# Output-projection weights prepared in the first MLP's second product instead of at the end of attention

## The chip, the cores and the metric

The kernel runs on one core of one Trainium2 chip. The metric is device microseconds of one execution: 2729.65 us in the median of three runs (2724.99 to 2732.59). One further execution was profiled. All times below are microseconds from the start of that execution's span unless they are called times of runs.

## The reference

Two post-norm residual layers over x of 1024 tokens x 1024 channels, f32. Layer 0 mixes tokens with a chunked gMLP, layer 1 with dilated attention in three patterns; each is followed by a squared-ReLU MLP. Every part is modulated by a conditioning vector c.

```python
for i in range(DEPTH):                      # DEPTH = 2
    shift, scale, gate = ada_mod(c, ada_w[i, 0], ada_b[i, 0])
    h = x * (1.0 + scale) + shift
    y = mixer_a(h, ...) if i == 0 else mixer_b(h, w_qkv, w_out, slopes)
    x = layer_norm(ALPHA * x + gate * y, ln_g[i, 0], ln_b[i, 0])
    shift, scale, gate = ada_mod(c, ada_w[i, 1], ada_b[i, 1])
    h = x * (1.0 + scale) + shift
    y = jnp.square(jax.nn.relu(h @ w_up)) @ w_down
    x = layer_norm(ALPHA * x + gate * y, ln_g[i, 1], ln_b[i, 1])

def mixer_b(h, w_qkv, w_out, slopes):       # 16 heads of 64, patterns (128,1) (512,4) (2048,16)
    ...
    outs, lses = one dilated_branch per pattern
    wts = softmax(stack(lses), axis=0)[..., None]
    o = sum(wts * stack(outs), axis=0)      # the merge
    return o.reshape(B, S, 1024) @ w_out
```

`w_out` of layer 1 (1024 x 1024) is what the change is about. Since `gate * (o @ w_out)` is `o @ (w_out * gate)`, its columns can be multiplied by the gate row beforehand.

## The kernel before

**Products.** Each f32 product runs as three matmuls of a rounded part (hi) and a rest (lo): hi x hi, hi x lo, lo x hi. An operand is split by `split`: ScalarE (ACT) casts to hi (line 102), VectorE (DVE) subtracts to get lo (line 103). The MLPs' products are cut into quarters and combined into seven products.

**Stages**, by the timeline: conditioning and gMLP mixer until about 365; first MLP, up product (psua to psuc) until 678.9; its second product (psd, line 955) until about 975; projection of the values (psv) until 1377; attention until 2033; the rest of the output projection (psoc, psod, psoe) until 2096; second MLP until the end.

**The second product of an MLP** (in `mlp`, with `load_step`, `prepare` and `matmuls`) is a loop over 56 steps of 24 matmuls (7 products x 8 pairs of k). Loads are issued three steps ahead, splits (lhi, llo of the left operand, rhi, rlo of the right one) two steps ahead. In between DVE takes up other work: differences of weight blocks that are held (heldt, heldr), and the residual acc, which is read back and multiplied and added to by the norm's rows (lines 300, 301). `x_tile` hands out 128x512 buffers from a ring.

**Attention** treats the 16 heads as 8 pairs (hp) x 3 patterns (g = 2, 1, 0): 24 groups of 8 slots, each slot of two half slots. A function decorated with `at(slot, pos, rank)` or passed to `in_half` is called when the planner comes to that half slot; between these calls matmuls of the q and k projections (psq, psk) and, at the end, of the output projection (psoa, psob) are dealt out. Per group: scores sc (line 1447), maxima and exponentials p (1467, 1469), transposes pT (1500), split into pThi and pTlo, product with the values pv (1527), evicted and added to oT (1536, 1537).

**The merge** of a pair joins its three patterns. `factors` computes weights from the maxima and sums (mm, ma, mal, lines 1590 to 1602) and stores them (w_dram), `spread` reads them back over the partitions as rows bc, and small steps scale (1623), add (1627) and cut (split into oTs, the left operand of the output projection). The last pair's merge runs in `go_on`, between psoc's and psod's matmuls; psod's last matmuls of each group (k = 7) and psoe need it.

**The output projection's weights** are 8 units of 128 x 1024 (wo). `staged_unit` loads one raw, multiplies it by the gate row (DVE, 1712), and splits it (ACT 102, DVE 103), for units 0 to 5 at set slots near the end of attention, for 6 and 7 in `go_on`.

**Order.** Every engine works through its own queue in order. SP's queue issues most DMAs; POOL's issues a few; an instruction that waits holds up what is behind it on its queue. A scheduler may move instructions on an engine, except those marked `tc.keep_in_program_order` ("pinned"), which keep their order among themselves.

Of the kernel before, what the change touches and what calls it, by code (L numbers as in the profile page):

```python
# [35 lines left out]
def trunk(ctx: ExitStack, tc: tile.TileContext, x, c, ada_w, ada_b, ln_g, ln_b, a_w_in, a_b_in,  # L36
# [615 lines left out]

    LEFT = {1: 0, 2: 1, 4: 2, 5: 3, 6: 4, 7: 5, 3: 6}
# [9 lines left out]
    def mlp(j, before, ahead=iter(())):  # L663
# [14 lines left out]
        with ExitStack() as ph:  # L678
# [324 lines left out]

            last_p = order[-1]
# [4 lines left out]
            with ExitStack() as pa:  # L1009
# [5 lines left out]
                for n, (p, kp) in enumerate(steps):  # L1015
# [35 lines left out]
                    if n == 4 * NT and j == 3:  # L1051
                        res.affine(j)
                    if p == last_p and kp > 0:
                        next(between, None)
# [3 lines left out]
                for m in range(4):  # L1058
                    for kp in range(tail, KP):
                        matmuls(last_p, kp, ms=[m], pinned=True)  # L1060
                    evict(last_p, m)()
                    res.finish(m, (1,))
                    if j == 3:
                        res.result(m, m == 3)
            spsum.close()
# [206 lines left out]
    def attention(form):  # L1272
# [5 lines left out]
        with ExitStack() as ph:  # L1278
# [104 lines left out]
            def attend(n, oT_of):  # L1383
# [6 lines left out]
                @at(base + 1, 0)  # L1390
# [178 lines left out]
            def merge(hp, oTs):  # L1569
# [15 lines left out]
                @at(*((base + 4, 0) if hp < N_PAIRS - 1 else (base + 1, 0)))  # L1585
                def factors():
# [3 lines left out]
                    in_order(V.tensor_tensor(m[:], nm[:, 0], nm[:, 1], op=ALU.min))  # L1590
# [15 lines left out]
                @at(*((base + 4, 1) if hp < N_PAIRS - 1 else (base + 1, 0)))  # L1606
# [39 lines left out]
                for n, f in enumerate(steps):  # L1646
                    n = pace * n + 18
                    at(base + n // 2, n % 2)(f)
# [44 lines left out]
            def pinned_split(hi, lo, src):  # L1693
                for x_ in split(hi, lo, src):
                    tc.keep_in_program_order(x_)

            @at(last_group - 13, 0)
            def gate_row():
                ending["gate"] = vec.tile([P, D], F32, name="gate_2", tag="oT", bufs=4)
                nc.sync.dma_start(ending["gate"][:], gate_dram[2].partition_broadcast(P))  # L1700

            def staged_unit(k, load, gate, ready):
                box = {}

                @at(last_group + load[0], load[1])
                def load_raw():
                    box["raw"] = wts.tile([P, D], F32, name=f"wo_{k}_raw", tag="raw", bufs=2)
                    nc.sync.dma_start(box["raw"][:], b_w_out[0, k * P : (k + 1) * P, :])

                @at(last_group + gate[0], gate[1])  # L1710
                def apply_gate():
                    tc.keep_in_program_order(V.tensor_tensor(box["raw"][:], box["raw"][:], ending["gate"][:], op=ALU.mult))

                def split_raw():
                    hi, lo = (wts.tile([P, D], F32R, name=f"wo_{k}_{m}", tag=f"w{m}")[:] for m in ("hi", "lo"))
                    pinned_split(hi, lo, box["raw"][:])
                    ending["units"][k] = hi, lo

                if ready is None:
                    return split_raw  # L1720
                at(last_group + ready[0], ready[1])(split_raw)

            staged_unit(0, (-14, 0), (-12, 0), (-11, 0))
            staged_unit(1, (-13, 0), (-11, 1), (-10, 1))
            staged_unit(2, (-11, 0), (-10, 0), (-9, 0))
            staged_unit(3, (-10, 1), (-9, 1), (-8, 0))
            staged_unit(4, (-2, 0), (2, 0), (8, 0))
            staged_unit(5, (-1, 0), (4, 0), (8, 1))
            late = [staged_unit(6, (9, 0), (11, 1), None), staged_unit(7, (9, 1), (12, 1), None)]
# [48 lines left out]
            def go_on():  # L1778
# [4 lines left out]
                for f in late:  # L1783
                    f()
# [73 lines left out]
```

## Time and profile before

| what | value |
|---|---|
| runs | 2729.65 us median (2724.99 to 2732.59), 3 runs |
| the profiled execution's own time | 2727.96 us |
| its span | 2726.2 us, 36911 instructions |
| mean granted TensorE clock | 0.995 |
| PE busy | 2658.8 us, 98% |
| DVE, ACT busy | 1989.8 us (73%), 1377.1 us (51%) |
| DMA | 487.98 MB, mean 179 GB/s |

The span runs from the first to the last instruction; 1.8 us of the execution lie around it. Busy shares are averages over stages that differ, so the prediction reads stretches of 25 us, and in them the idle time of PE. A row of a timeline gives start, duration, engine, line, operation, output<-inputs and, in brackets, how long the engine stood idle before it and what ended that. A row of the chain gives start, duration and the work on the path that ended last. bc, wo, pTlo and the like are the program's tile names.

### The profile page before, as it was taken

How to read it: one execution, taken by the hardware profiler on the slowest of the kernel's cores; microseconds unless marked ns; L12 is line 12 of the kernel's file. 1: busy time of each engine (PE TensorE's matmuls, PEld its weight loads, DVE VectorE, ACT ScalarE, POOL GpSimd, SP SyncE). 2: the span in 40 equal slices, each digit the busy share in tenths (PEclk: the TensorE clock that was granted, in tenths of full speed). 3: DMA queues.
4: the chain of work that ended last, by engine and by line, in shares of the span. 5: the costliest groups of instructions: out<-in, count | busy, mean ns of one | idle time of the engine just before them, and what ended most of it. 6: DMA issues, size and time to landing. Idle time of an engine off the chain costs nothing.

```text
span 2726.2 us, 36911 instructions
## 1 busy us (share of the span) xinstructions
PE 2658.8 (98%) x13242; PEld 2196.3 (81%) x13242; DVE 1989.8 (73%) x3594; ACT 1377.1 (51%) x2593; POOL 97.0 (4%) x161
## 2 busy tenths in 40 slices
PE   6999999999999999999999999999999999999998
PEld 5788888887888878888888888888777788878886
DVE  6787698787867778555557767777768966577877
ACT  3354375555443464434436666666655655554332
POOL 1000000000000000111110000000010000000000
PEclk9999999999999999999999999999999999999999
DMA  7534346667936545655565554555672654485562
GB/s 263 159 118 134 116 140 224 227 214 257 333 131 194 195 155 193 212 186 182 178 210 153 155 140 129 132 144 139 193 183 105 202 189 159 149 311 192 171 207 86
DMA packets 332572, 487.98 MB, mean 179 GB/s; under 512 B 50988, under 2 KB 176340, under 8 KB 332388
## 3 DMA queue, kind: packets, MB, share of 16 engines
q1 hardware_dynamic: 318564, 435.29, 50.3%
q0 software_dynamic: 13824, 50.34, 5.2%
q8 instruction: 104, 1.70, 0.3%
q14 instruction: 80, 0.66, 0.1%
HBM read 357.01 MB, written 128.53 MB: 178 GB/s over the span
## 4 chain that ended last, share of the span: by engine, by line
PE 77%; DVE 12%; DMA 6%; ACT 3%; issue 2%; SPq 1%; DVEq 0%; ACTq 0%
PE psd L955 22%; PE psv L1257 13%; PE psua L796 7%; PE psq L1358 6%; PE psk L1358 6%; DMA adaw<-in_ada_w_dram 3%; PE psuc L796 3%; PE psd_wout L389 3%; PE psu L368 3%; PE pv L1527 3%; PE sc L1447 2%; PE psv L470 2%; PE psub L796 2%; DVE adaacc L128 1%; DVE left L103 1%
## 5 line engine op out<-in xcount | busy, mean ns | idle before, releaser
L796 PE MATMUL psua<-right,left 128*128 128x512 f32 x1536 | 363.4, 390 | 0.3
L955 PE MATMUL psd<-rhi,lhi 128*128 128x512 f32 x896 | 349.9, 390 | 3.0 <-ACT part L827 3.0
L955 PE MATMUL psd<-rlo,lhi 128*128 128x512 f32 x896 | 349.6, 390 | 0.2
L955 PE MATMUL psd<-rhi,llo 128*128 128x512 f32 x896 | 349.2, 390 | 0.0
L796 PEld LDWEIGHTS psua<-right,left 128*128 128x128 f32 x1536 | 287.1, 188 | 61.7 <-DVE right L103 1.4
L1469 ACT ACTIVATE p<-p,stat 128x128 f32<-128x128 f32 (+1 forms) x384 | 168.7, 441 | 107.8 <-DVE stat L1467 104.7
L955 PEld LDWEIGHTS psd<-rhi,lhi 128*128 128x128 f32 x896 | 168.6, 188 | 39.1 <-ACT part L827 3.9
L955 PEld LDWEIGHTS psd<-rlo,lhi 128*128 128x128 f32 x896 | 168.5, 188 | 35.9 <-DVE rlo L103 1.1
L955 PEld LDWEIGHTS psd<-rhi,llo 128*128 128x128 f32 x896 | 168.6, 188 | 35.0
L796 PE MATMUL psuc<-right,left 128*128 128x512 f32 x768 | 187.2, 390 | 0.0
L128 DVE SCALAR_TENSOR_TENSOR adaacc<-adaw,silu_c,adaacc 128x512 f32<-128x512 f32 x168 | 128.5, 775 | 55.0 <-DMA adaw<-in_ada_w_dram 54.6
L796 PEld LDWEIGHTS psuc<-right,left 128*128 128x128 f32 x768 | 143.5, 188 | 30.0 <-DVE right L103 0.4
L103 DVE TENSOR_TENSOR pTlo<-pT,pThi 128x512 fp32r<-128x512 f32 (+1 forms) x160 | 99.3, 621 | 75.1 <-ACT pThi L102 74.1
L103 DVE TENSOR_TENSOR left<-ws,left 128x512 fp32r<-128x512 f32 x128 | 87.8, 688 | 71.5 <-ACT left L102 69.7
L103 DVE TENSOR_TENSOR llo<-lraw,lhi 128x1024 fp32r<-128x1024 f32 x112 | 136.4, 1218 | 0.8 <-ACT lhi L102 0.8
L102 ACT CAST left<-ws 128x512 fp32r<-128x512 f32 x128 | 79.1, 620 | 99.1 <-DVE ws L717 87.8
L1358 PE MATMUL psk<-form_L,wqk_hi 128*128 128x512 f32 x384 | 127.0, 412 | 0.0
L1358 PE MATMUL psq<-form_L,wqk_hi 128*128 128x512 f32 x384 | 126.4, 410 | 0.0
L102 ACT CAST rhi<-rraw 128x1024 fp32r<-128x1024 f32 x48 | 50.6, 1053 | 139.6 <-issue 113.7
L1257 PE MATMUL psv<-vrhi,form_S 128*128 128x512 f32 x384 | 119.9, 390 | 0.6 <-ACT vrhi L102 0.4
L102 ACT CAST lhi<-lraw 128x1024 fp32r<-128x1024 f32 x112 | 117.4, 1048 | 3.5 <-PE psua L796 3.5
L1467 DVE CUSTOM_DVE_ANT_0 p<-sc,bias 128x128 f32<-128x128 f32 (+1 forms) x384 | 113.6, 346 | 6.7 <-PE sc L1447 5.8
(326 smaller groups left out, 6094.4 us busy)
## 6 DMA issues: line engine op xcount, KB each, us to landing
lraw<-forms SPq DMA_DIRECT2D x112, 512.0 KB
adaw<-in_ada_w_dram SPq DMA_DIRECT2D x192, 256.0 KB
up<-in_mlp_w_up_dram SPq DMA_DIRECT2D x64, 512.0 KB
forms<-s SPq DMA_DIRECT2D x128, 256.0 KB
rraw<-in_mlp_w_down_dram SPq DMA_DIRECT2D x64, 512.0 KB
forms<-part SPq DMA_DIRECT2D x96, 256.0 KB
v<-vs POOLq DMA_DIRECT2D x48, 512.0 KB, 3.7
vraw<-in_b_w_qkv_dram SPq DMA_DIRECT2D x42, 512.0 KB
```

The lines of the kernel that those rows point to most:

```text
L102: first = A.copy(hi, src) if hi_engine is A else hi_engine.tensor_copy(hi, src)
L103: return first, lo_engine.tensor_tensor(lo, src, hi, op=ALU.subtract)
L128: ins = V.scalar_tensor_tensor(acc[:], raw[:], silu_c[:, k : k + 1], acc[:], ALU.mult, ALU.add)
L368: T.matmul(dst, s[a], m[b], start=(n == 0), stop=(n == last))
L389: T.matmul(p[:], stat[a][:, k, o : o + P], u[b][:, w], start=n == 0, stop=n == count - 1)
L796: T.matmul(acc, w[:, a, k, :], right[p][:, b, k, :], start=p in (1, 2, 5) and k + a + b == 0, stop=k == 3 and a == 1, skip_group_check=True)
L955: ins = T.matmul(sums[kind, m][:], l[a][:, k, m * P : (m + 1) * P], r[b][:, k, :], start=p in (1, 5, 2, 3) and kp + k + a + b == 0, stop=k ...
L1257: T.matmul(acc, rows[:, m * P : (m + 1) * P], cols_, start=p in (1, 2, 5) and kp + k + a + b == 0, stop=kp == 1 and k == 1 and a == 1, ski ...
L1358: T.matmul(p[:], wu[a][:, k * P : (k + 1) * P], h_op(k, half, b), start=k + c_ == 0, stop=k == KD - 1 and c_ == 2)
L1467: V.tensor_tensor_reduce(out=pr, in0=banks[e][:, sl], in1=st["bias"][:, width - w :], scale=-0.125, scalar=3e38, op0=ALU.add, op1=ALU.min, ...
L1469: A.activation(pr, pr, AF.Exp, bias=nm, scale=-1.0, accum_out=l)
L1527: T.matmul(pvs[b][:, q0 % HALF : q0 % HALF + w_], stt, x_[:, o_ : o_ + w_], start=not begun[b], stop=left[b] == 0, skip_group_check=True)
```

## The change

1. **Weights.** `output_weights`, called in each step of the first MLP's second product, treats the output weights in 16 halves (pieces) of 128 x 512: a load into an `x_tile`, two or more steps later the multiplication by the gate row (pinned), the split, and two stores by POOL's queue to a DRAM buffer `wo_parts`. One piece starts every 2.75 steps or so, from step 3 on. The gate row is loaded once as two half rows.
2. **Units.** In attention, `load_unit` replaces `staged_unit`: it reads hi and lo of a unit, already split, from `wo_parts` (2 x 512 KB), at half slots before and in the last group; unit 3 into the tiles of the raw projection weights, unit 7 into a tile of the values, the others into the split weights' tiles.
3. **Values.** `load_v` is called two slots earlier.
4. **Merge.** The scale, add and cut steps of pairs 0 to 6 come four half slots later.
5. **Last merge.** `factors` and `spread` of pair 7 are called one half slot later, and the first operation of every `factors` is pinned.

```diff
+    wo_dram = dram.tile([N_PAIRS, P, 2, 2, HALF], F32, name="wo_parts")
...
+            across, pieces, begun = [], deque((k, dh) for k in range(N_PAIRS) for dh in range(2)), deque()
+            def output_weights(n):
+                if n == 1:
+                    for dh in range(2):
+                        across.append(work.tile([P, HALF], F32, name=f"gate_2_{dh}", tag="h"))
+                        nc.sync.dma_start(across[dh][:], gate_dram[2, dh * HALF : (dh + 1) * HALF].partition_broadcast(P))
+                if n > 2 and pieces and (n - 2) * 16 // 44 > N_PAIRS * 2 - len(pieces) - 1:
+                    k, dh = pieces.popleft()
+                    raw = x_tile(f"wo_raw_{k}_{dh}")
+                    nc.sync.dma_start(raw[:], b_w_out[0, k * P : (k + 1) * P, dh * HALF : (dh + 1) * HALF])
+                    begun.append((n, k, dh, raw))
+                elif begun and begun[0][0] < n - 1:
+                    _, k, dh, raw = begun.popleft()
+                    hi = x_tile(f"wo_hi_{k}_{dh}")
+                    tc.keep_in_program_order(V.tensor_tensor(raw[:], raw[:], across[dh][:], op=ALU.mult))
+                    split(hi[:].bitcast(F32R), raw[:].bitcast(F32R), raw[:])
+                    for i, t in enumerate((hi, raw)):
+                        nc.gpsimd.dma_start(wo_dram[k, :, dh, i, :], t[:])
...
+                    if j == 1:
+                        output_weights(n)
...
-                @at(base + 1, 0)
+                @at(max(0, base - 1), 0)
                 def load_v():
...
-                @at(*((base + 4, 0) if hp < N_PAIRS - 1 else (base + 1, 0)))
+                @at(*((base + 4, 0) if hp < N_PAIRS - 1 else (base + 1, 1)))
                 def factors():
...
-                    in_order(V.tensor_tensor(m[:], nm[:, 0], nm[:, 1], op=ALU.min))
+                    tc.keep_in_program_order(V.tensor_tensor(m[:], nm[:, 0], nm[:, 1], op=ALU.min))
...
-                @at(*((base + 4, 1) if hp < N_PAIRS - 1 else (base + 1, 0)))
+                @at(*((base + 4, 1) if hp < N_PAIRS - 1 else (base + 1, 1)))
                 def spread():
...
-                    n = pace * n + 18
+                    n = pace * n + 22
...
-            def staged_unit(k, load, gate, ready):
...
-            staged_unit(0, (-14, 0), (-12, 0), (-11, 0))
...
-            late = [staged_unit(6, (9, 0), (11, 1), None), staged_unit(7, (9, 1), (12, 1), None)]
+            def load_unit(k):
+                if k == 7:
+                    t = qp.tile([P, 2, D], F32R, name="wo_7", tag="v")
+                    ending["units"][k] = tuple(t[:, i, :] for i in range(2))
+                else:
+                    ending["units"][k] = tuple(wts.tile([P, D], F32R, name=f"wo_{k}_{m}", tag="raw" if k == 3 else f"w{m}", bufs=2 if k == 3 else 4)[:] for m in ("hi", "lo"))
+                for i, t in enumerate(ending["units"][k]):
+                    nc.sync.dma_start(t.rearrange("p (d c) -> p d c", c=HALF).bitcast(F32), wo_dram[k, :, :, i, :])
+
+            for k, half_slot in ((3, -34), (0, -32), (1, -30), (2, -27), (4, -15), (7, 11), (5, 17), (6, 18)):
+                in_half(2 * last_group + half_slot, 4)(lambda k=k: load_unit(k))
```

What this moves on the engines is shown at three places. Names carry their indices: oT_7_2 is pair 7, pattern 2; pTlo_15_2_0 head 15, pattern 2, part 0; bc_6_2 the factors of pair 6 for pattern 2; the long number behind is a tile's count.

DVE, where pair 6 is merged while pair 7's pattern 1 begins (1963 to 1977 in the profile), before:

```order
L1623 TENSOR_TENSOR bc_6_2_18240<-oT_6_2_17475,bc_6_2_18240 128x512 x2
L1537 TENSOR_TENSOR oT_7_2_18445<-oT_7_2_18445,pv_14_2_0_18316 64x512
L1537 TENSOR_TENSOR oT_7_2_18445<-oT_7_2_18445,pv_14_2_1_18317 64x512
L103 TENSOR_TENSOR pTlo_15_2_0_18451<-pT_15_2_0_18426,pThi_15_2_0_18450 128x512
L1467 ISA p_14_1_3_18454,stat_7_1_18332<-sc_14_1_1_18431,bias_14_1_18333 128x256
L1467 ISA stat_7_1_18332 128x1
L1467 ISA p_15_1_3_18457,stat_7_1_18332<-sc_15_1_1_18432,bias_15_1_18335 128x256
L1467 ISA stat_7_1_18332 128x1
L1712 TENSOR_TENSOR wo_2_raw_18254<-wo_2_raw_18254,gate_2_18135 128x1024
L103 TENSOR_TENSOR wo_1_lo_18288<-wo_1_raw_18137,wo_1_hi_18287 128x1024
L1623 TENSOR_TENSOR bc_6_1_18237<-oT_6_1_17766,bc_6_1_18237 128x512
L103 TENSOR_TENSOR wo_2_lo_18297<-wo_2_raw_18254,wo_2_hi_18296 128x1024
```

and after:

```order
L1563 TENSOR_TENSOR oT_7_2_18566<-oT_7_2_18566,pv_14_2_1_18444 64x512
L103 TENSOR_TENSOR pTlo_15_2_0_18572<-pT_15_2_0_18547,pThi_15_2_0_18571 128x512
L1493 ISA p_14_1_3_18575,stat_7_1_18458<-sc_14_1_1_18552,bias_14_1_18459 128x256
L1493 ISA stat_7_1_18458 128x1
L1493 ISA p_15_1_3_18578,stat_7_1_18458<-sc_15_1_1_18553,bias_15_1_18461 128x256
L1493 ISA stat_7_1_18458 128x1
L1493 ISA p_14_1_5_18581,stat_7_1_18458<-sc_14_1_1_18552,bias_14_1_18459 128x256
L1493 ISA stat_7_1_18458 128x1
L1493 ISA p_15_1_5_18584,stat_7_1_18458<-sc_15_1_1_18553,bias_15_1_18461 128x256
L1493 ISA stat_7_1_18458 128x1
L1649 TENSOR_TENSOR bc_6_2_18382<-oT_6_2_17607,bc_6_2_18382 128x512 x2
L1563 TENSOR_TENSOR oT_7_2_18566<-oT_7_2_18566,pv_15_2_0_18604 64x512
```

The scaling of pair 6 (bc_6_2) stood ahead of pTlo_15_2_0 and now stands behind it and two more rounds of p; the weights' multiply and splits are gone.

DVE, the last pTlo operations of attention and the factors of the last merge (2024 to 2033), before:

```order
L103 TENSOR_TENSOR pTlo_15_0_0_19016<-pT_15_0_0_19010,pThi_15_0_0_19015 128x512
L1590 TENSOR_TENSOR mm_7_19082<-mst_7_18992 128x16
L1591 TENSOR_TENSOR mm_7_19082<-mm_7_19082,mst_7_18992 128x16
L1594 TENSOR_TENSOR ma_7_19085<-mm_7_19082,mst_7_18992 128x16 x3
L1597 TENSOR_TENSOR mal_7_19090<-ma_7_19085,mst_7_18992 128x48
...
L103 TENSOR_TENSOR pTlo_15_0_1_19042<-pT_15_0_1_19031,pThi_15_0_1_19041 128x512
L1600 RECIPROCAL mal_7_19090<-mal_7_19090 128x16
L103 TENSOR_TENSOR wo_4_lo_19046<-wo_4_raw_18613,wo_4_hi_19045 128x1024
L103 TENSOR_TENSOR pTlo_15_0_2_19061<-pT_15_0_2_19055,pThi_15_0_2_19060 128x512
L103 TENSOR_TENSOR wo_5_lo_19065<-wo_5_raw_18637,wo_5_hi_19064 128x1024
L103 TENSOR_TENSOR pTlo_15_0_3_19079<-pT_15_0_3_19074,pThi_15_0_3_19078 128x384
L1602 TENSOR_TENSOR ma_7_19085<-ma_7_19085,mal_7_19090 128x16 x3
```

and after:

```order
L103 TENSOR_TENSOR pTlo_15_0_0_19136<-pT_15_0_0_19130,pThi_15_0_0_19135 128x512
L1563 TENSOR_TENSOR oT_7_0_19156<-oT_7_0_19156,pv_14_0_1_19071 64x512
L103 TENSOR_TENSOR pTlo_15_0_1_19162<-pT_15_0_1_19151,pThi_15_0_1_19161 128x512
L103 TENSOR_TENSOR pTlo_15_0_2_19177<-pT_15_0_2_19171,pThi_15_0_2_19176 128x512
L1563 TENSOR_TENSOR oT_7_0_19156<-oT_7_0_19156,pv_15_0_0_19165 64x512
L103 TENSOR_TENSOR pTlo_15_0_3_19195<-pT_15_0_3_19190,pThi_15_0_3_19194 128x384
L1616 TENSOR_TENSOR mm_7_19206<-mst_7_19112 128x16
L1617 TENSOR_TENSOR mm_7_19206<-mm_7_19206,mst_7_19112 128x16
L1620 TENSOR_TENSOR ma_7_19209<-mm_7_19206,mst_7_19112 128x16 x3
```

The splits of weight units 4 and 5 are gone from between the pTlo operations, and the whole computation of the factors follows the last pTlo.

At the same place SP's queue after the change (wo_parts is the new DRAM buffer, up the second MLP's weights):

```order
L1608 DMA mst_7_19112<-st_dram_11367 128x4x8
L1726 DMA wo_5_lo_19181<-wo_parts_107 128x2x512
L1726 DMA wo_5_hi_19180<-wo_parts_107 128x2x512
L1726 DMA wo_6_hi_19198<-wo_parts_107 128x2x512
L1726 DMA wo_6_lo_19199<-wo_parts_107 128x2x512
L1630 DMA w_dram_11368<-ma_7_19209 128x2x8 x3
L1637 DMA bc_7_1_19225<-w_dram_11368 64x1024 x2
```

Where four unit loads of 512 KB now stand ahead of the factors' store, there were two loads of raw weights of 512 KB (units 6 and 7).

DVE in the second product, about its seventh step, after the change (gate_2 is the gate row, wo_raw_0_0 the first piece, llo and rlo the operands' splits):

```order
L103 TENSOR_TENSOR llo_1_5_0_6327<-lraw_1_5_0_6281,lhi_1_5_0_6326 128x1024
L300 TENSOR_TENSOR acc_1_6_6021<-acc_1_6_6021,lng_0_6137 128x1024
L301 TENSOR_TENSOR acc_1_6_6021<-acc_1_6_6021,lnb_0_6139 128x1024
L103 TENSOR_TENSOR rlo_1_5_0_6332<-heldt_1_0_6031,rhi_1_5_0_6331 128x1024
L1022 TENSOR_TENSOR wo_raw_0_0_6220<-wo_raw_0_0_6220,gate_2_0_6146 128x512
L103 TENSOR_TENSOR llo_1_5_1_6378<-lraw_1_5_1_6322,lhi_1_5_1_6377 128x1024
L103 TENSOR_TENSOR wo_raw_0_0_6220<-wo_raw_0_0_6220,wo_hi_0_0_6335 128x512
L719 TENSOR_TENSOR heldt_1_0_6031<-heldr22_1_0_6033,heldt_1_0_6031 128x1024
```

The multiply and the lo part of a piece stand between the operands' splits; before, the same rows stood there without L1022 and the split of wo_raw.

30 lines of the change are left out of this document (1 added, 29 removed).

## The prediction

> **What bounds the kernel now.** I read the page's busy shares first, then the busy time of each engine in 25 us stretches, the waits of PE and DVE in the attention stage, the chain that ended last, and last the timelines of PE, DVE and SP at the places found.
>
> ```profile
> PE 2658.8 (98%) x13242; PEld 2196.3 (81%) x13242; DVE 1989.8 (73%) x3594; ACT 1377.1 (51%) x2593; POOL 97.0 (4%) x161
> ```
>
> PE is busy for 98% of the span, so no change can win more than the few tens of us in which PE is idle or runs at a reduced clock. The stretches say where these are (columns: us; busy PE, PEld, DVE, ACT, POOL; granted clock; DMA share; GB/s).
>
> ```profile
> 700.00:725.00 25.00, 25.00 (x112) 20.71 (x111) 23.86 (x22) 11.24 (x14) 0.00 (x0) 1.00 0.93 325
> 725.00:750.00 25.00, 25.00 (x112) 20.67 (x111) 23.95 (x22) 8.97 (x9) 0.00 (x0) 1.00 0.93 323
> 775.00:800.00 25.00, 25.00 (x112) 20.71 (x111) 12.54 (x11) 8.40 (x9) 0.00 (x0) 1.00 0.30 100
> 850.00:875.00 25.00, 25.00 (x112) 20.65 (x111) 24.77 (x28) 8.60 (x9) 0.00 (x0) 1.00 0.59 185
> ...
> 1475.00:1700.00 225.00, 221.84 (x1492) 185.32 (x1491) 159.79 (x487) 141.31 (x420) 7.10 (x19) 1.00 0.53 142
> 1925.00:1950.00 25.00, 25.00 (x182) 21.31 (x181) 14.28 (x56) 14.41 (x47) 0.60 (x2) 1.00 0.63 183
> 1950.00:1975.00 25.00, 20.41 (x130) 16.66 (x128) 20.48 (x51) 15.63 (x45) 0.81 (x2) 0.93 0.80 241
> 1975.00:2000.00 25.00, 22.69 (x128) 18.68 (x127) 15.31 (x40) 12.97 (x36) 3.46 (x5) 0.93 0.93 238
> 2025.00:2050.00 25.00, 22.79 (x102) 18.57 (x101) 21.66 (x38) 7.92 (x12) 0.85 (x1) 0.86 0.61 141
> ```
>
> The first four rows lie in the first MLP's second product: PE never pauses, while DVE and the DMA engines are close to full until 750. The last four lie at the end of attention. There PE loses 3.16 us in 1475 to 1700, 4.59 + 2.31 = 6.9 us in 1950 to 2000 and 2.21 us in 2025 to 2050. A mean clock of 0.93 over 25 us is 3.5 us at half rate, so up to 1.75 us lost in each of two stretches; 0.86 is 7 us at half rate, 3.5 us lost. Who is waited for (engine, line, releaser: us in total, times, longest; DVE first, then PE):
>
> ```profile
> DVE bc L1623 <- DMA bc<-w_dram: 16.2, 6, 3.7
> ...
> PE pv L1527 <- DVE pTlo L103: 7.6, 10, 2.3
> PE pv L1527 <- ACT pThi L102: 3.9, 3, 3.3
> ```
>
> DVE stands in front of the merge factors bc, which come by DMA, and PE's pv product then waits for what stands behind it on DVE. The PE and DVE timelines show both kinds of stall:
>
> ```profile
> 1967.71 0.33 PE L1527 MATMUL pv<-pThi,v 128*128 128x128 f32 x1 [3.26 <-ACT pThi L102]
> 1978.22 0.33 PE L1527 MATMUL pv<-pTlo,v 128*128 128x128 f32 x1 [2.27 <-DVE pTlo L103]
> 2030.47 0.39 PE L1527 MATMUL pv<-pTlo,v 128*128 128x256 f32 x1 [0.95 <-DVE pTlo L103]
> ...
> 1963.92 1.98 DVE L1623 TENSOR_TENSOR bc<-oT,bc 128x512 f32<-128x512 f32 x2 [1.97 <-DMA bc<-w_dram]
> 1976.36 1.21 DVE L1712 TENSOR_TENSOR wo_raw<-wo_raw,gate 128x1024 f32<-128x1024 f32 x1
> 1977.50 0.67 DVE L103 TENSOR_TENSOR pTlo<-pT,pThi 128x512 fp32r<-128x512 f32 x1
> ```
>
> At 1963.92 the merge of pair 6 waits for bc, and the oT add and pTlo stand behind it. At 1976.36 an output weight's gate multiply stands ahead of the pTlo that PE waits 2.27 us for.
>
> **The change part by part.** Durations are those of the profiled execution, 2727.96 us, which lies 1.69 us under the median of 2729.65; the sum is made against it.
>
> Output weights, what leaves attention's end:
>
> ```profile
> L1712 DVE TENSOR_TENSOR wo_raw<-wo_raw,gate x8: 1205/1218/1226, 1952.7 to 2036.2; 128x1024 f32<-128x1024 f32 x8
> L102 ACT CAST wo_hi<-wo_raw x8: 1044/1048/1058, 1953.9 to 2046.5; 128x1024 fp32r<-128x1024 f32 x8
> L103 DVE TENSOR_TENSOR wo_lo<-wo_raw,wo_hi x8: 1203/1216/1225, 1955.0 to 2049.8; 128x1024 fp32r<-128x1024 f32 x8
> ```
>
> That is 8 x (1.22 + 1.22) = 19.5 us of DVE and 8 x 1.05 = 8.4 us of ACT, all between 1952 and 2051. What arrives in the second product are the same elements as 16 halves:
>
> ```profile
> L103 DVE TENSOR_TENSOR left<-ws,left 128x512 fp32r<-128x512 f32 x128 | 87.8, 688 | 71.5 <-ACT left L102 69.7
> L102 ACT CAST left<-ws 128x512 fp32r<-128x512 f32 x128 | 79.1, 620 | 99.1 <-DVE ws L717 87.8
> v<-vs POOLq DMA_DIRECT2D x48, 512.0 KB, 3.7
> ```
>
> DVE takes 16 x 2 x 0.69 = 22 us and ACT 16 x 0.62 = 9.9 us, spread over about 240 us. In 700 to 750 that is some three pieces, 4 us of DVE where 2.2 us are free (50 - 23.86 - 23.95); the rest pushes acc and held-block operations, which no matmul waits for at once, into 775 to 800, where half of DVE is free. The 850 row (24.77) is as tight for one stretch. ACT has half its time. On SP's queue come 18 loads of 256 KB, on POOL's queue, idle in these rows, 32 stores of 256 KB. With reads and writes a piece moves 0.75 MB; five pieces before 750 are 3.75 MB, 11.5 us at the 325 GB/s of the 700 row, in a DMA system that is 93% busy. The transfers that a split waits for are issued three steps ahead, a step being 24 matmuls. Cost on PE: at least nothing (PE 25.00 in all rows, no split was the last to arrive); at most, 11.5 us less the two steps by which splits run ahead (2 x 24 x 0.227 = 10.9, the pitch from the psoe row below), and another 2 to 3 us if DVE also has to stand for a load: 0 to 3 us. I take 0.5, near the lower end, since PE never waited there. Later, unit loads read 8.4 MB instead of 4.2 + 0.5. The 1925 row (63% DMA) covers the early units; unit 2's 1 MB ahead of pair 6's statistics can make their bc later by 1 MB / 241 GB/s = 4 us, less than the next part gives.
>
> The merge two slots later (4 half slots; attention's 656 us hold some 200 slots, 3.1 to 3.4 us each, an estimate): DVE meets bc over 6 us after it did, and the longest wait was 3.7 us. So the six waits go. In 1475 to 1700 PE gets back between 0 and 3.16 us; I take 3.0, since the only stalls there stood behind bc.
>
> In 1950 to 2000 nothing of the weights and no bc wait is left ahead of pTlo. Up to 6.9 us idle plus the half-rate time in which PE was busy (1.75 us of the second stretch; the first coincides with the 3.26 us stall) come back, 8.65 us; at least the 3.26 + 2.27 us of the two named waits, 5.5 us. I take 7.8, close to the upper end, as both causes are gone, and leave 0.85 for short waits of the pT, pThi, pTlo, pv sequence. PE at half rate after a pause is in these rows; "TensorE: Matmul & The Clock Gate" of the Trainium skill, Part 1, says that the rate falls after an idle window of about 3.4 us and comes back after a busy one. By that rule the half-rate stretches go together with the stalls, and this row's sum would be 8.65 us and more; the trace agrees in the length (3.5 us per stretch) but shows a drop after a stall shorter than the window, so I do not count all of it.
>
> In 2025 to 2050 two casts of 1.05 us and two splits of 1.22 us stood between the last pTlo operations. The chain that ended last prices the clock:
>
> ```profile
> 2032.97 13.16 PE psoc L1756 x48
> 2046.13 19.84 PE psod L1756 x87
> 2084.89 10.91 PE psoe L1756 x48
> ```
>
> psoc and the last part of psoe are 48 matmuls each: 13.16 - 10.91 = 2.25 us at reduced clock (0.227 us per matmul at full rate). Recoverable are 2.21 + 3.5 = 5.7 us; at least nothing, if the chain of small operations keeps PE pausing and the rate low. I take 3.2, just over the middle.
>
> The last merge (pair 7), against this. From DVE's and SP's timelines:
>
> ```profile
> 2025.36 0.17 DVE L1590 TENSOR_TENSOR mm<-mst 128x16 f32<-128x16 f32 x1
> 2031.46 0.55 DVE L103 TENSOR_TENSOR pTlo<-pT,pThi 128x384 fp32r<-128x384 f32 x1
> 2031.93 0.34 DVE L1602 TENSOR_TENSOR ma<-ma,mal 128x16 f32<-128x16 f32 x3
> 2041.39 1.09 DVE L1623 TENSOR_TENSOR bc<-oT,bc 128x512 f32<-128x512 f32 x1
> 2048.64 2.35 DVE L103 TENSOR_TENSOR wo_lo<-wo_raw,wo_hi 128x1024 fp32r<-128x1024 f32 x2
> 2054.05 1.47 DVE L103 TENSOR_TENSOR oTs<-bc,oTs 128x512 fp32r<-128x512 f32 x2
> ...
> 2032.12 1.41 SPq L1604 DMA_DIRECT2D w_dram<-ma  x3
> 2036.49 3.68 SPq L1611 DMA_DIRECT2D bc<-w_dram  x6
> ```
>
> Call T the end of the last pTlo, 2032.0. Before, the factors were ready at T + 0.3, bc was used from T + 9.4 and the first oTs was cut at 2054.7 = T + 22.7. Now the factors start at T. Without the work between them they take some 3 us (2.3 us of small operations, one oT add of 0.69), so bc lands by T + 10.5 to T + 12.1 and DVE needs about 9.5 us from there (six scales, four of 1.0 and two of 0.6, 5.2; four adds of 0.6, 2.4; two splits of 0.6 and a cast of 0.6; wo_lo's 2.35 is gone): T + 20.0 to T + 21.6. psod's matmuls with weight unit 7 need the cut: psoc starts at T + 0.8, takes 10.9 at full rate, and 36 matmuls of psod come first, 8.2: T + 19.9. The stall is between 0 and 1.7 us, plus up to 2 if psoc's additions to acc stand in the way; I take 1.5. Moving load_v changes SP's order by one place: nothing.
>
> Sum: -3.0 - 7.8 - 3.2 + 0.5 + 1.5 = -12.0 us, 2716.0 on the profiled execution, 2717.7 on the median; I say 2717.
>
> **The rivals.**
> A: the last merge eats its gain. Units 5 and 6, 2 MB, are issued ahead of w_dram and bc, once psob's last matmul has run:
>
> ```profile
> L1756 PE MATMUL psob<-wo_hi,oTs x32: 389/397/497, 2007.1 to 2025.1; 128*128 128x512 f32 x32
> ```
>
> That is T - 6.5 (T - 4 with the stalls gone); 2.1 MB at 241 GB/s take 8.7 us, until T + 2 to T + 5, against w_dram at T + 3. If bc comes 2 us later still, and up's load and split, now ahead of the cut on DVE, take 2 more, the stall is 1.5 + 4 = 5.5: 2720 to 2722. For it: the cut has no slack. Against: the 325 GB/s row shows that the DMA system can be faster.
>
> B: the pauses stay though their releasers change, since pT, pThi, pTlo and pv follow each other on three engines anyway, and each pause keeps the rate low. Half of 7.8 + 3.2: 2722.5. For it: the 0.95 us wait of 2030.47 is of that size. Against: the two large waits have a bc or a weight in front.
>
> C: slower. The x tiles that hold the pieces come free only when a POOL store has landed (3.7 us for 512 KB above). SP then stands at the next piece's load, and the operand loads behind it on SP are late. It costs nothing while a piece's delay stays under the 10.9 us of lead, and decides from (12.0 + 8.2) / 16 = 1.3 us of PE per piece. If every piece cost 2 us, +32 - 12 = +20: 2749. If only the five before 750, where DMA is at 93%: 2727. On the DMA ceiling, "DMA: Bandwidth & Descriptors" of the Trainium skill, Specifications, gives about 358 GB/s per core between HBM and SBUF; the trace agrees with its 325, so by that rule the five early pieces have to push other transfers back by 10 to 11 us, which speaks against the change.
>
> **How the numbers follow.** About 0.3% (8.2 us) is what a measurement of this kernel can tell from no change. The forecast has 0.54, all faster (2711 to 2721.5). A has 0.15: 0.10 within 0.3%, 0.05 faster. B has 0.13: 0.12 within, 0.01 faster. C has 0.16: 0.11 slower, 0.05 (its weaker form) within. 0.02 is left for a gain beyond. That makes faster 0.62, same 0.27, slower 0.11. The lowest case, all of 3.16 + 10.4 + 5.7 us with no cost, is 2708.7; the upper end takes in A, B and C's weaker form: 2708 to 2729.
>
> **What would show it.** Right: no wait of DVE's bc for DMA over 0.5 us before the last merge; PE over 24 us busy in each 25 us from 1925 to 2025, clock 1.00; no wo operation on DVE or ACT after 1000; psoc near 10.9 us; PE at 25.00 in the stretches from 700 to 950. Wrong: waits of psd for rlo, llo or a load (C); a gap inside psod with oTs as its releaser (A); pv still waiting 2 us and more for pTlo at the end of attention (B).

## The result and the profile after

The changed kernel takes 2716.92 us in the median of five runs (2713.02 to 2719.31). The kernel before took 2729.1 us in the median of five runs (2724.99 to 2732.59). The ratio is 0.9951, with a 95% interval of 0.9935 to 0.9966: some 12 us, 0.5%, faster. The profiled execution took 2717.79 us, of which its span is 2716.1 us.

Busy time per stretch, after (columns as in the prediction: us; PE, PEld, DVE, ACT, POOL; granted clock; DMA share; GB/s):

```profile
700.00:725.00 25.00, 25.00 (x112) 20.71 (x111) 23.75 (x23) 12.14 (x15) 1.32 (x2) 1.00 0.94 332
725.00:750.00 25.00, 25.00 (x112) 20.71 (x111) 22.45 (x22) 11.20 (x13) 2.16 (x4) 1.00 0.93 328
775.00:800.00 25.00, 25.00 (x112) 20.69 (x111) 20.06 (x21) 9.84 (x11) 2.70 (x5) 1.00 0.63 215
850.00:875.00 25.00, 25.00 (x111) 20.60 (x111) 24.01 (x28) 10.47 (x11) 1.09 (x2) 1.00 0.69 229
1475.00:1700.00 225.00, 224.53 (x1515) 188.77 (x1514) 160.56 (x494) 143.78 (x430) 7.10 (x19) 1.00 0.52 141
1925.00:1950.00 25.00, 25.00 (x183) 21.37 (x182) 16.35 (x63) 14.71 (x49) 1.17 (x4) 1.00 0.70 213
1950.00:1975.00 25.00, 25.00 (x167) 21.12 (x166) 15.61 (x49) 13.73 (x44) 1.17 (x2) 1.00 1.00 302
1975.00:2000.00 25.00, 24.29 (x156) 20.25 (x156) 15.56 (x51) 18.52 (x55) 4.01 (x6) 1.00 0.89 217
2000.00:2025.00 25.00, 23.91 (x143) 19.70 (x143) 14.62 (x39) 12.99 (x28) 3.27 (x4) 1.00 0.86 205
2025.00:2050.00 25.00, 21.13 (x85) 16.57 (x84) 17.91 (x30) 3.95 (x6) 0.00 (x0) 0.93 0.62 175
```

The second product (first four rows) carries the extra work and PE never pauses. The end of attention is mended: PE is busy for 49.29 us of 1950 to 2000 at full clock, where it was busy for 43.10 at 0.93. 2025 to 2050, which now holds psoc and psod, is not mended: PE is busy for 21.13 us, and the clock of 0.93 is one stretch of half rate. The waits of 1377 to 2075 name the cause:

```profile
DVE bc L1649 <- DMA bc<-w_dram: 9.0, 2, 5.5
...
PE psod L1756 <- ACT oTs L102: 3.5, 1, 3.5
...
PE pv L1553 <- DVE pTlo L103: 1.0, 3, 0.4
```

The waits of pv for pTlo fell from 7.6 to 1.0 us, and those for pThi from 3.9 us to almost nothing. In their place stands one new wait inside psod, for the cut oTs of the last merge. The chain that ended last (start, us, what) runs through that merge, from its store and read through DRAM to the cut:

```profile
2021.87 5.71 DMA w_dram<-ma
2027.59 0.49 SPq L1637
2028.13 4.02 DMA bc<-w_dram
2032.38 0.87 issue
2033.25 0.67 DVE acc L1769
2034.34 0.50 issue
2034.84 1.28 DVE acc L1769 x2
...
2042.97 12.99 PE psod L1756 x49
```

To follow where the time went I read eight marks out of each kernel's trace: the first psq matmul, the first of psoc, of psod and of psoe, and on DVE the last pTlo (T is its end), the ready factors (ma), the first scale with bc, and the end of the last cut.

| us | psq to psoc | psoc | psod | psq to psoe | T to ma | ma to bc | bc to cut |
|---|---|---|---|---|---|---|---|
| before | 655.7 | 13.2 | 21.9 | 690.8 | 0.3 | 9.1 | 14.1 |
| after | 639.6 | 10.9 | 29.3 | 679.9 | 3.0 | 10.7 | 11.3 |

Attention and psoc gain 16.1 + 2.3 = 18.4 us; psod gives 7.4 of it back. What remains is 10.9 us. The spans differ by 10.1 us, because psq began 2.3 us later than before and what follows the first psoe took 1.5 us less. The late start is scatter: the second product of the first MLP starts between 672.0 and 679.1 us in the traces of this document.

### The profile page after: what moved, and what is told of

It is laid out like the page before. It is cut to its first block, busy times and chain, and to the rows that moved or that the text cites. A ratio compares the mean times of both kernels' runs of the same rounds, so it can differ in the third digit from the quotient of the medians.

```text
span 2716.1 us, 37099 instructions
## 1 busy us (share of the span) xinstructions
PE 2655.5 (98%) x13242; PEld 2193.5 (81%) x13242; DVE 1993.0 (73%) x3610; ACT 1378.4 (51%) x2601; POOL 114.9 (4%) x193
## 4 chain that ended last, share of the span: by engine, by line
PE 76%; DVE 12%; DMA 6%; ACT 3%; issue 2%; SPq 0%; DVEq 0%; ACTq 0%
PE psd L957 22%; PE psv L1283 13%; PE psk L1384 6%; PE psq L1384 6%; PE psua L798 6%; DMA adaw<-in_ada_w_dram 3%; PE psd_wout L389 3%; PE pv L1553 3%; PE psuc L798 3%; PE psu L368 3%; PE sc L1473 3%; PE psv L470 2%; DVE adaacc L128 2%; DVE left L103 1%; PE pT L1526 1%
## 5 line engine op out<-in xcount | busy, mean ns | idle before, releaser
L102 ACT CAST pThi<-pT 128x512 fp32r<-128x512 f32 (+1 forms) x160 | 84.6, 530 | 60.4 <-PE pT L1526 43.3
```

The lines of the kernel that those rows point to most:

```text
L102: first = A.copy(hi, src) if hi_engine is A else hi_engine.tensor_copy(hi, src)
```

## The experiments

Twelve runs follow, ten edited kernels, one of them twice, and the changed kernel once more, in groups that each shared a chip and its runs of the kernel before. "Ratio" is the time against the kernel before on the same chip, with its 95% interval.

| run | median us | ratio | psq to psoc | psod | psq to psoe | ma to bc |
|---|---|---|---|---|---|---|
| e_factors0 | 2713.61 | 0.9959 [0.9944, 0.9973] | 644.7 | 23.2 | 679.6 | 9.7 |
| e_merge18 | 2712.9 | 0.9951 [0.9936, 0.9966] | 640.7 | 28.7 | 680.3 | 10.5 |
| e_weights_only | 2714.01 | 0.9951 [0.9934, 0.9967] | 653.5 | 23.2 | 689.4 | 10.2 |
| e_merge_only | 2724.66 | 0.9998 [0.9988, 1.0007] | 654.7 | 21.9 | 690.0 | 9.3 |
| e_swap | 2710.15 | 0.9932 [0.9919, 0.9945] | 639.3 | 25.0 | 675.3 | 8.3 |
| e_poolq | 2718.37 | 0.9961 [0.9948, 0.9974] | 639.3 | 30.5 | 680.7 | 10.9 |
| e_swap_mst | 2709.97 | 0.9928 [0.9916, 0.9941] | 637.9 | 25.5 | 674.4 | 8.1 |
| e_dve2 | 2713.67 (one run) | | 639.1 | 29.5 | 679.5 | 10.6 |
| e_dve_back | 2710.84 | 0.9946 [0.9933, 0.9960] | 643.8 | 24.6 | 680.9 | 9.8 |
| e_act_back | 2714.43 | 0.9952 [0.9937, 0.9967] | 640.6 | 28.3 | 680.0 | 10.6 |
| e_after | 2712.13 | 0.9947 [0.9935, 0.9960] | 638.5 | 29.8 | 679.3 | 11.2 |
| e_swap_b | 2708.77 | 0.9937 [0.9922, 0.9951] | 638.6 | 24.3 | 673.9 | 7.6 |

### Which part of the change is worth what

**The factors' slot undone** (the change without its part 5):

```diff
-                @at(*((base + 4, 0) if hp < N_PAIRS - 1 else (base + 1, 1)))
+                @at(*((base + 4, 0) if hp < N_PAIRS - 1 else (base + 1, 0)))
                 def factors():
...
-                    tc.keep_in_program_order(V.tensor_tensor(m[:], nm[:, 0], nm[:, 1], op=ALU.min))
+                    in_order(V.tensor_tensor(m[:], nm[:, 0], nm[:, 1], op=ALU.min))
```

> The changed kernel with part 5 undone: the last merge's factors and spread one half slot earlier, first operation not pinned. Theory (late factors plus the unit loads ahead of them cost the psod pause): the factors are ready some 2.5 us earlier against psoc's start, so psod with its pause shrinks from 29.3 us to 25 to 27 us, psoc starts within 1 us of where it did, time 2713 to 2715. Rival (the pause is set by the DMA backlog of units 5 and 6 alone): psod stays at 29 us. Second rival (the small operations between the pTlo cost pv as much as they win): psoc's start moves 2 us later and the time stays at 2717.

The wait did not vanish, it moved. In the timelines of DVE and PE (start, us, engine and line, operation, idle time before it and what ended that) DVE now stands in front of the statistics mst with the last pTlo operations behind it, and PE with it:

```profile
2016.63 0.18 DVE L1616 TENSOR_TENSOR mm<-mst 128x16 f32<-128x16 f32 x1 [5.41 <-DMA mst<-st_dram]
...
2018.94 0.69 PE L1553 MATMUL pv<-pThi,v 128*128 128x256 f32 x2 [5.91 <-ACT pThi L102]
```

psod shrinks to 23.2 us, and attention and psoc grow by nearly as much (5.1 and 0.7 us); first psq to first psoe is 679.6 us against 679.9. In the median this part is worth nothing that was measured. The two kernels without it scatter most (19.4 us over ten runs here, 14.5 us over the four of e_weights_only, 6.3 us over five of the changed kernel).

**The merge's slot undone** (the change without part 4), and **parts 1 to 3 alone** (this edit together with the one above, so without parts 4 and 5):

```diff
-                    n = pace * n + 22
+                    n = pace * n + 18
```

> The changed kernel with part 4 undone: the merge steps 4 half slots earlier, as before. Theory (DVE waits for bc, and pv behind it): PE's idle time in 1475 to 1700 returns from 0.5 to about 3 us, a pause of about 3 us returns near 1960, the stretch from attention's first projection to psoc grows from 639.6 to about 645 us, time 2722 to 2724. Rival (the weights on DVE made the merge late, not its slot): 639 to 641 us, time 2717.

> The kernel before with the weights' part alone (parts 1 to 3): merge and last merge as before. Theory (the parts add up): the stretch to psoc is about 645 us instead of 655.7, since the weights' stalls near 1976 and 2030 go and the bc stalls stay; psod is 25 to 27 us instead of 21.9 (units 5 and 6 still load ahead of the last factors); second product of the first MLP as before, 313 to 315 us; time 2720 to 2723. Rival (the weights give everything): stretch of 640 us, time 2714.

**Part 4 alone**, the reverse edit in the kernel before:

> The kernel before with part 4 alone: merge steps 4 half slots later, weights as before. Theory: bc waits go, the weights' waits stay: the stretch to psoc shrinks from 655.7 to 648 to 650 us, psod stays at 22 us, time 2721 to 2724. Rival (weights then stand where bc stood, and the wait only changes its name): 653 to 656 us, time 2727 to 2729.

Every kernel that has parts 1 to 3 is faster, by 0.4 to 0.7%; these parts are called the weights' part here, and no run separates the values' earlier load (part 3) from it. The merge's slot alone is worth nothing (0.9998), and taking it out of the change costs nothing. In e_merge_only the waits changed their names: pv waits 2.2 us for pTlo instead of 7.6, but psoa now waits for a weight's split,

```profile
PE psoa L1756 <- DVE wo_lo L103: 1.9, 1, 1.9
```

and from 1950 to the start of psod 17.1 us run at half rate, where it was 13.7. e_merge18's waits (us in total, times, longest) and its DVE at pair 6 say why the bc waits were the wrong thing to count:

```profile
DVE bc L1649 <- DMA bc<-w_dram: 17.1, 7, 5.3
...
PE pv L1553 <- DVE pTlo L103: 2.1, 4, 0.8
...
1960.08 2.07 DVE L1649 TENSOR_TENSOR bc<-oT,bc 128x512 f32<-128x512 f32 x2 [2.05 <-DMA bc<-w_dram]
```

The longest of the seven waits, 5.3 us, is the last merge's, and psod stands behind it as in the changed kernel. The other six make 11.8 us, against 16.2 us for six in the kernel before, yet PE waits 2.1 us for pTlo instead of 7.6. The wait for pair 6 is as long as it was (2.05 us, before 1.97), and PE, which stood 3.26 us there, does not stand at all. In 1475 to 1700, where the prediction gave the slot 3.0 us, PE is busy for 223.07 us with the weights' part alone, 222.73 with the slot alone and 224.53 with both, from 221.84 before: the slot is worth 0.9 to 1.5 us there.

e_weights_only's profile is of the slowest of its four runs (2724.34 us; 2709.8 to 2724.34). Beside the wait for mst that e_factors0 shows too, it has one late in attention that the others have at 0.3 to 1.4 us or not at all:

```profile
1997.54 1.65 PE L1473 MATMUL sc<-bk,bq 64*128 64x256 f32 x12 [4.36 <-DMA bk<-qk]
```

So its stages in the table, which take in both waits, look like those of before while its median does not; of its profile only what lies ahead of 1975 is used here.

### What PE waited for at the end of attention

My reading at this point was DVE's load: 19.5 us of weight operations between 1952 and 2051. Two runs put such work back into the changed kernel, at the places that the weights had: twelve DVE operations of 1.22 us, or six ACT copies. Both use the gate row's tile, which takes one of the four oT buffers, as it did before; nothing reads what they write.

```diff
+            @at(last_group - 13, 0)
+            def gate_row():
+                ending["gate"] = vec.tile([P, D], F32, name="gate_2", tag="oT", bufs=4)
+                nc.sync.dma_start(ending["gate"][:], gate_dram[2].partition_broadcast(P))
+            def filler():
+                t = ending["gate"][:]
+                tc.keep_in_program_order(V.tensor_tensor(t, t, t, op=ALU.max))    # e_dve_back
+                tc.keep_in_program_order(A.copy(t, t))                            # e_act_back
...
+                at(last_group + a_, b_)(filler)
```

> The changed kernel with DVE's occupation by the weights put back alone at attention's end: 12 operations of 128x1024 on a tile that nothing reads (the maximum of the gate row with itself), pinned, at the rows where the weights' gate multiplies and splits of units 0 to 5 stood; no cast on ACT, no raw loads. Theory (a pTlo behind a weight's operation on DVE makes pv late, and pairs of them drop the clock): the stretch from attention's first projection to psoc grows from 639.6 us by 6 to 12 us, time 2720 to 2726. Rival (DVE's 15 us are absorbed, and what made PE wait before was a load or a cast that those operations waited for): 640 to 643 us, time unchanged.

> The same for ACT alone: 6 copies of 128x1024 on a tile that nothing reads at the rows of the weights' casts. Theory (ACT had room; the casts cost only where one stands ahead of a pThi late in the last group): the stretch grows by 0 to 2 us. Rival (the casts made pThi late, which was the largest single wait): 4 us and more.

DVE's share of work came back and the stalls did not. The stretches of e_dve_back:

```profile
1950.00:1975.00 25.00, 22.96 (x147) 18.75 (x144) 18.73 (x51) 13.75 (x45) 2.59 (x4) 1.00 0.92 281
1975.00:2000.00 25.00, 23.62 (x157) 19.41 (x156) 18.86 (x52) 17.69 (x50) 2.62 (x4) 1.00 0.80 176
```

DVE is busy for 37.59 us of these 50, more than before (35.79), and PE for 46.58 at full clock, against 43.10 at 0.93. First psq to first psoc grows by 4.1 us over the changed kernel's 639.6, or by 5.2 over the 638.5 of its second trace (e_after, on the same chip), not by 16. The six ACT copies cost 1.0 or 2.1 us. So DVE's occupancy, put back with the merge in its new slot, gives back a quarter to a third of what attention gained. It reaches PE by way of ACT: from 1964.05 on DVE's scales, fillers and other work follow each other without a pause, ACT stands 4.49 us for statistics behind them (until 1970.41), and PE 1.77 us for ACT (until 1972.80). And e_dve_back's psod is 4.7 us shorter (ma to bc 9.8 us), so that its total is not above the changed kernel's.

What else was different is seen on ACT. Its timeline in the kernel before, at the 3.26 us stall that the prediction quotes:

```profile
1965.99 1.07 ACT L1536 COPY oT<-pv 64x512 f32<-64x512 f32 x2 [2.69 <-DVE bc L1623]
1967.08 0.58 ACT L102 CAST pThi<-pT 128x512 fp32r<-128x512 f32 x1
```

ACT could not copy pv into pair 7's oT before DVE had scaled pair 6's oT by bc: in the code four tiles share that ring, the gate row was one of them, and the new tile took the old one's place. The cast pThi stood behind that copy on ACT, and PE's pv behind the cast. So PE waited for bc over a buffer and ACT's queue, not over the pTlo behind bc on DVE. With the merge four half slots later and the weights left as they were (e_merge_only) the same wait of ACT is still there, though PE waits only 0.6 us near it (at 1972.13, for DVE's oT):

```profile
1968.85 1.07 ACT L1536 COPY oT<-pv 64x512 f32<-64x512 f32 x2 [2.46 <-DVE bc L1623]
```

In the changed kernel and in e_merge18, where the gate row is gone, ACT has no such wait. In e_dve_back and e_act_back, where the buffer is taken again but the merge is later, it is 0.5 us. No run changed the buffer alone, so its price is read from the one stall (3.26 us and the half-rate stretch behind it, some 5 us). That leaves most of the 16 us. At the other stall, of 2.27 us until 1978.22, the kernel before shows what the prediction said of it. DVE has no pause from 1966.60 on, and three scales and the gate's multiply (1976.36) stand right ahead of the pTlo of 1977.50; the casts of pThi had ended at 1972.49. ACT stood for the same multiply, but its own next operation then had to wait for PE, so this cast held up nothing that the trace shows:

```profile
1974.16 2.27 DVE L1623 TENSOR_TENSOR bc<-oT,bc 128x512 f32<-128x512 f32 x3
...
1977.60 1.05 ACT L102 CAST wo_hi<-wo_raw 128x1024 fp32r<-128x1024 f32 x1 [2.58 <-DVE wo_raw L1712]
1981.22 0.58 ACT L1765 COPY acc<-psoa 128x512 f32<-128x512 f32 x1 [2.57 <-PE psoa L1756]
```

So one of the two named stalls is DVE's load, merge and weights together, and the other a buffer and ACT's queue. The fillers of e_dve_back also lack the chain of a unit, handed from the load to DVE, ACT, DVE and psoa's matmul: psoa waited for its end 0.3 us in the kernel before and 1.9 us in e_merge_only. No run put that chain back with its real dependencies: how the rest divides between the chain, the loads and the clock stays open.

### What the second product can carry

Each piece gets two more DVE operations of 0.69 us; what they write is overwritten by the split:

```diff
                     tc.keep_in_program_order(V.tensor_tensor(raw[:], raw[:], across[dh][:], op=ALU.mult))
+                    for _ in range(2):
+                        V.tensor_tensor(hi[:], raw[:], across[dh][:], op=ALU.mult)
```

> The changed kernel with two more 128x512 DVE operations per piece of the weights in the first MLP's second product (their output is overwritten): 32 more, 22 us of DVE. Theory (DVE's other work there can slip, splits run ahead): the second product stays at 313 to 315 us, PE at 25.00 per 25 us. Rival C of the prediction (a piece costs PE time as soon as DVE is full): 1.3 us per piece and more, 330 us and over.

```profile
750.00:775.00 25.00, 25.00 (x112) 20.71 (x111) 25.00 (x26) 10.47 (x13) 1.09 (x2) 1.00 0.64 235
775.00:800.00 25.00, 25.00 (x112) 20.68 (x112) 24.93 (x28) 12.04 (x14) 3.23 (x6) 1.00 0.59 201
850.00:875.00 25.00, 25.00 (x112) 20.62 (x111) 25.00 (x30) 9.35 (x10) 1.09 (x2) 1.00 0.66 222
```

With DVE at 100% for whole stretches of 25 us PE still does not pause, and the product takes as long as in the other kernels (314.8 us from the start of its first to that of its last matmul; 313 to 315 elsewhere). A run with twice the weights' DVE work here costs nothing.

### What the last merge waits for

Four loads of 512 KB (units 5 and 6) stand ahead of the factors' store on SP's queue. SP's timeline, after:

```profile
2014.58 0.52 SPq L1726 DMA_DIRECT2D wo_lo<-wo_parts  x1
2015.19 1.28 SPq L1726 DMA_DIRECT2D wo_hi<-wo_parts  x2
2016.52 1.13 SPq L1726 DMA_DIRECT2D wo_lo<-wo_parts  x1
2021.41 1.40 SPq L1630 DMA_DIRECT2D w_dram<-ma  x3
2027.59 3.69 SPq L1637 DMA_DIRECT2D bc<-w_dram  x6
```

Between issuing the store and issuing the read that needs it lie 6.18 us; before, with two loads ahead, 2032.12 to 2036.49, 4.37 us. Two edits tell a backlog in the DMA engines from a place in SP's queue. The first loads unit 5 early into the tile of the values that unit 7 had, and unit 7 after bc's reads, so that one unit and not two lies ahead:

```diff
-                if k == 7:
-                    t = qp.tile([P, 2, D], F32R, name="wo_7", tag="v")
+                if k == 5:
+                    t = qp.tile([P, 2, D], F32R, name="wo_5", tag="v")
...
-            for k, half_slot in ((3, -34), (0, -32), (1, -30), (2, -27), (4, -15), (7, 11), (5, 17), (6, 18)):
+            for k, half_slot in ((3, -34), (0, -32), (1, -30), (2, -27), (4, -15), (5, 11), (6, 17), (7, 20)):
```

with the last bc's reads and unit 7's loads pinned in that order.

> The changed kernel with the roles of weight units 5 and 7 exchanged: unit 5 is loaded early into the values' tile, and unit 7 (needed last) only behind the last merge's bc on SP's queue, so 1 MB instead of 2 MB stand ahead of the factors' store. Theory (the psod pause is late factors plus DMA backlog): the store lands some 1.5 to 2 us sooner than its 6.2 us, the pause in psod falls from 4.6 to 2 to 3 us, psod from 29.3 to 26 to 28 us, time 2 to 3 us under the changed kernel's. Rival (three DRAM round trips set it, whatever else is in the queue): psod stays at 29 us.

The second leaves the loads and sends the store and the read by POOL's queue:

```diff
-                        nc.sync.dma_start(w_dram[hp, g]...
+                        (nc.sync if hp < N_PAIRS - 1 else nc.gpsimd).dma_start(w_dram[hp, g]...
```

(and the same for the reads of bc).

> The changed kernel with the last merge's factors stored and read back by POOL's queue instead of SP's, behind which the unit loads stand. Theory (backlog in SP's own queue): psod 26 to 28 us. Rival (the DMA engines themselves are busy, or POOL's issue is slower): psod 29 to 31 us.

e_swap was run once more, on one chip with the changed kernel as it is:

> The changed kernel itself, for a comparison on one chip with the kernel with units 5 and 7 exchanged: 0.994 to 0.996 of the kernel before, and 2 to 5 us above the exchange.

> The kernel with units 5 and 7 exchanged once more, beside the changed kernel on the same chip: 0.993 of the kernel before. If the gain of the exchange was chance, both stand at 0.995.

SP's timeline in e_swap_b, and POOL's in e_poolq:

```profile
2012.31 0.52 SPq L1728 DMA_DIRECT2D wo_lo<-wo_parts  x1
2012.92 0.56 SPq L1728 DMA_DIRECT2D wo_hi<-wo_parts  x1
2019.83 2.04 SPq L1630 DMA_DIRECT2D w_dram<-ma  x3
2022.83 3.69 SPq L1637 DMA_DIRECT2D bc<-w_dram  x6
```

```profile
2017.63 2.22 POOL L1630 DMA_DIRECT2D w_dram<-ma  x3 [6.75 <-issue]
2023.46 1.07 POOL L1637 DMA_DIRECT2D bc<-w_dram  x2 [3.61 <-DMA w_dram<-ma]
```

With 1 MB ahead the store's trip takes 3.00 us instead of 6.18 (3.53 in e_swap, 6.49 in e_after); on POOL's queue, with 2 MB ahead, 5.83. The busy share of the 16 DMA engines, in tenths per 0.55 us, from 2014 in the changed kernel:

```profile
DMA  9156386899999999999994100007796799999989
```

and from 2012 in e_swap_b:

```profile
DMA  9735957789999995320200799999999998999999
```

After, the engines are full until the 21st digit, 2025.5, four us after the store was issued, and then nearly idle until bc's reads start. In e_swap_b they are full only until 2020.2, when the store has just been issued. It is the transfers in the DMA engines that the store stands behind, not the entries in SP's queue. The Trainium skill, "DMA: Bandwidth & Descriptors", section "Issuing engines are not separate DMA queues", says that transfers started by different engines run on the same 16 DMA engines and interleave there; these three numbers agree.

In e_poolq SP issued loads of up while POOL still issued the reads of bc, and psod's longest pause is 5.4 us. In e_swap and e_swap_b it falls from the changed kernel's 3.4 us to 1.0 and 0.3, the clock does not fall there, and first psq to first psoe falls from 679.3 us (e_after) to 673.9 (e_swap_b). The ratio is 0.9932 and 0.9937: faster than both kernels in the median, and in the trace where it should be. Against the changed kernel on the same chip, 2708.77 to 2712.13 us, the intervals overlap, so the run times alone do not settle these 3 us.

**The statistics by POOL as well.** The last mst read waits for a store to land, and loads of bq and bk stand behind it on SP's queue (the bk wait above):

```diff
-                        nc.sync.dma_start(st[:, g]...
+                        (nc.sync if hp < N_PAIRS - 1 else nc.gpsimd).dma_start(st[:, g]...
```

> The exchange of units 5 and 7 together with the last merge's statistics (mst) read by POOL's queue, so that SP's queue no longer stands at the wait for their store with the last group's bq and bk loads behind it. Theory: beside the shorter psod, PE's wait of sc for bk (0.7 us in the changed kernel, 4.4 us in the run with the weights alone) goes; time 2709 to 2712 on a chip where the changed kernel takes 2713 to 2715, and less scatter. Rival: bk's wait comes from the full DMA engines and stays.

The waits for bk are gone from the list; the time is e_swap's (2709.97 and 2710.15 us).

## Why the prediction was right or wrong

The time said was 2717.0 us and 2716.92 was measured. Part of that is errors that cancel.

- **End of attention, -7.8 and -3.2.** Right in place, too small. Together with the -3.0 that is -14.0 for attention and psoc; 18.4 us were measured. In 1950 to 2000 PE's idle time gave 6.2 us (49.29 less 43.10) and the two half-rate stretches some 3.2, so 9.4 instead of 7.8: the prediction let the first of them coincide with the 3.26 us stall and left it out, but it began 1.6 us after the stall had ended, with PE busy for 3.07 of its 3.41 us. 1475 to 1700 gave 2.7. By difference some 6 us are left for the end of attention and psoc, where 3.2 were taken out of 5.7. psoc came out at 10.93 us, as written. Of the signs, PE was above 24 us busy in the three stretches from 1925 to 2000 and short of it in the fourth (23.91).
- **The cause within it.** The prediction said that weights and bc waits on DVE stood ahead of pTlo. The weights' part is indeed the whole gain (e_weights_only 0.9951, e_merge_only 0.9998), but the step from "DVE busy ahead of pTlo" to "PE waits" failed as the general account: twelve DVE operations put back cost 4.1 to 5.2 us. Of the two named stalls the 2.27 us one went as written, the 3.26 us one through an oT buffer and ACT's queue.
- **The merge two slots later, -3.0.** Failed at "the only stalls there stood behind bc". The slot is worth 0.9 to 1.5 us in that stretch and nothing measurable in the total. The sign "no wait of bc over 0.5 us before the last merge" was wrong too: one of 3.4 us is left, and no matmul waits behind it.
- **Second product, +0.5.** It was 0: PE at 25.00 us in every stretch, even with twice the work. Rival C (a piece that costs PE over 1.3 us) found nothing to stand on. Nor are the 358 GB/s that it quotes a ceiling in these traces: from 2021.7 to 2025.0 the changed kernel moved 406 GB/s.
- **The last merge, +1.5.** Mis-sized: psod grew by 7.4 us. The factors took the predicted time (3.0 us, some 3). bc was used at T + 13.7 instead of T + 10.5 to 12.1, because the DRAM trip stands behind 2 MB of unit loads. From there to the cut's end passed 11.3 us instead of 9.5: the chain shows three additions to acc, 1.95 us, between the scales, which the prediction allowed for and did not count. PE's pause of 3.45 + 0.42 us brought a half-rate stretch, about 1.7 us. The 7.4 us also hold a wait of 1.2 us for acc in front of psoe; every kernel with the weights' part has it, e_swap_b too, so it does not come from the pause. The late bc and the pause are rival A's mechanism, and its sign, the gap inside psod with oTs as its releaser, is in the trace. Rival A as a whole did not come true (2720 to 2722), since attention gained 4.4 us more than said.
- **Rival B**, pauses that stay: refuted for 1950 to 2000 by 49.29 of 50 us at full clock.

## What to carry to other kernels

A wait that one engine shows is not what it costs the next one: e_merge18 kept 11.8 of 16.2 us of DVE's waits ahead of the last merge and PE hardly noticed, while a tile that waited for its buffer held up another queue and with it PE. So before a stall is priced, follow who waits behind it, over buffers as well as over operations. When large loads are moved, look at which small store-and-read trip through DRAM comes after them: 1 MB less ahead of it was worth 4 to 5 us of psod here, and another issuing engine was worth nothing.

## What the hardware showed that was not expected

- The granted clock halves behind pauses of PE, for 3.41 us, twice that, or three times that (10.24 us in e_merge_only, from 2024.25). A stretch of the changed kernel, three of the kernel before and one of e_dve_back:

```profile
2042.90:2046.30 3.40, 3.33 (x8) 2.66 (x9) 2.52 (x6) 1.90 (x2) 0.00 (x0) 0.50 0.93 303
```

```profile
1969.29:1972.70 3.41, 3.07 (x13) 2.47 (x12) 3.41 (x4) 3.15 (x8) 0.00 (x0) 0.50 0.24 71
1979.53:1982.94 3.41, 3.41 (x11) 2.73 (x11) 3.41 (x15) 1.45 (x4) 0.00 (x0) 0.50 1.09 390
2030.73:2037.56 6.83, 6.26 (x18) 4.91 (x18) 5.48 (x10) 0.81 (x2) 0.00 (x0) 0.50 0.58 169
```

```profile
2015.37:2018.78 3.41, 3.41 (x11) 2.73 (x11) 3.11 (x14) 0.82 (x2) 0.00 (x0) 0.50 1.03 284
```

  The first three begin 1.1, 1.6 and 1.3 us after the matmuls had begun again behind pauses of 3.45, 3.26 and 2.27 us. The length of one pause does not decide it: pauses of 1.77 us (e_dve_back, until 1972.80) and 1.0 us (e_swap) were followed by none, while three waits of 0.28, 0.60 and 0.87 us between 2011.5 and 2015.1 were (the last row, e_dve_back). "TensorE: Matmul & The Clock Gate" of the Trainium skill, Part 1, lets the rate fall after an idle window of about 3.4 us; the length of the stretches agrees, the drop after 2.27 us does not.
- A store of 24 KB to DRAM held up the read behind it for 3.0 us (e_swap_b), 4.4 us (before) or 6.2 us (after), by what had been issued ahead of it.
- DVE at 25.00 of 25 us (e_dve2, 750 to 775) held up neither PE nor the stores of 256 KB by POOL's queue: those of 750 to 800 landed 2.6 to 5.0 us after their issue, in the changed kernel 3.3 to 5.3 us.
